# Start addresses of weight and moving tiles in a two-layer fp32 decoder kernel: distance 0 for products of 512 columns, 64 for products of 256

## The chip, the core and the metric

The kernel runs on one core of one Trainium2 chip. The metric is the device time of one execution in microseconds (us); lower is better. Of the kernel before, three runs are known: 1990.70, 1990.41 and 1990.72 us, median 1990.7.

## The reference

Two layers over 512 tokens of width 1024, all in float32. Each layer is a half-step gated feed-forward network (FFN), a mixer, a second FFN and a gated per-layer input. The mixer of layer 0 is a convolution module, that of layer 1 a sparse attention. Cut to what matters here:

```python
for i in range(2):
    x = x + 0.5 * swiglu(rms_norm(x, ffn1_norm[i]), ffn1_w_gate[i], ffn1_w_up[i], ffn1_w_down[i])
    h = rms_norm(x, mix_norm[i])
    x = x + (conformer_conv(h, ...) if i == 0 else nsa_mixer(h, ...))
    x = x + 0.5 * swiglu(rms_norm(x, ffn2_norm[i]), ffn2_w_gate[i], ffn2_w_up[i], ffn2_w_down[i])
    gate = sigmoid(rms_norm(x, ple_norm[i]) @ ple_w_gate[i])
    x = x + gate * (p[i] @ ple_w_in[i])
return rms_norm(x, final_norm)

def swiglu(x, wg, wu, wd):                 # x 512x1024, wg and wu 1024x2816, wd 2816x1024
    return (silu(x @ wg) * (x @ wu)) @ wd
```

## The kernel before

Everything is kept transposed: a tile has 128 features in its partitions and the 512 tokens along a row. A float32 value is split into a high part, rounded to the type that TensorE multiplies in one pass (fp32r), and a low part, the rest. A product of float32 matrices is then three matmuls, issued by `mm3` (lines 361 to 365): weights high with moving high (L363), weights high with moving low (L364), weights low with moving high (L365). Each matmul is a weight load of 128x128 (PEld in the profile) and the pass of the moving operand over it (PE). The load for the next matmul runs during the pass of this one.

There are two widths of moving operand.

- **Products of 512 columns**: one matrix block against all tokens. The down projections of the FFNs (moving tiles `hid`), the first two gate and up blocks of each FFN, the convolution module's projections (moving tiles `s`, and `tw` for the second one), the per-layer input (`px`, `zp`), the attention's projections (`s`, and `e` for part of its output), and the attention's own scores (`kt` against weights `q`) and weighted sums (`t` and `ect` against weights `v` and `vc`).
- **Products of 256 columns**: the other gate and up blocks. `pairs` (its copies and additions are L509 and L510; `ffn` calls it) works on two blocks of 128 output features at once with a seven-product scheme, in which a product takes sums of blocks and half of the tokens. Per pair of blocks the names `s`, `c`, `e`, `d` stand for the four kinds of weights: the block itself, its two sums, and the sum `s1hl`, which is kept in a tile of its own. The moving operands are halves of `s` or `px` tiles (columns 0 to 255, or 256 to 511). In the final stage (`final`) the last three blocks of the last gate also go by halves of 256 columns.

An FFN runs in three parts of 8, 8 and 6 blocks (`PARTS`). Each part is gate and up, then the down projection of these blocks into the accumulated result. So on TensorE a stretch of 256-column products is followed by one of 512-column products, three times per FFN; the first part of an FFN begins with four plain 512-column blocks.

Weights come from memory by DMA into `raw` tiles of 128x1024, are split by ScalarE (`wh`, L299) and VectorE (`wl`, L301), and stay in a ring of five pairs of tiles (`HLB`). A tile holds eight 128-column blocks; a matmul reads one block, 512 bytes of each partition.

**Where the tiles lie.** A pool's tiles lie one after another in each partition, in the order in which their tags are first used, and every start is a multiple of 32 bytes. For this text the *distance* of a matmul is the start of its weights minus the start of its moving operand, modulo 256 bytes. (The words of the change count it the other way, moving minus weights: their 192 is 64 here.) As blocks are 512 bytes apart and halves 1024, all products of a kind of tile have one distance. In the kernel before three paddings are set by hand (`PAD_SLOTS`, `PAD_PHASE`, `PADS`), and the starts modulo 256 are: `wh`, `wl` 192; `s`, `px` 0; `hid` 192; `s1hl` 64; `tw` 224; `zp` 96; `t` 0 against `v` 224. That gives these distances:

| products | columns | matmuls | distance before | distance after |
|---|---|---|---|---|
| `s`, `px` with `wh`, `wl` | 256 | 5,904 | 192 | 64 (144 of the final stage: 0) |
| `px` with `s1hl` | 256 | 960 | 64 | 64 |
| `hid` with `wh`, `wl` | 512 | 2,112 | 0 | 0 |
| `s`, `px` with `wh`, `wl` | 512 | 1,656 | 192 | 0 |
| `tw` with `wh`, `wl` | 512 | 192 | 224 | 0 |
| `zp` with `wh`, `wl` | 512 | 96 | 96 | 0 |
| `e` with `wh`, `wl` | 512 | 96 | eight values, 0 to 224 | 0 |
| `t` with `v`; `ect` with `vc` | 512 | 160; 32 | 224; 0 | 0; 0 |
| `kt` with `q` | 512 | 64 | 160 or 32 | 0 |

The engines take their instructions in the order of the program, as the scheduler has laid it down; each waits for its operands by semaphores.

Of the kernel before, what the change touches and what calls it, by code (L numbers as in the profile page):

```python
# [21 lines left out]
TAPS = 31  # L22
X_W1, WARM = 4, 18
OUTS = 2
PAD_SLOTS, PAD_PHASE = 16, 48
PADS = {"s1hl": 16, "G": 48, "hid": 48}
CONV_FIN = 0
PE_LATE = (3, 4, 5)
FIN_PRI = 100
# [16 lines left out]
EB = 9  # L46
# [151 lines left out]
class Kern:  # L198
    def __init__(self, ctx, tc, aps):
        self.ctx, self.tc, self.nc = ctx, tc, tc.nc  # L200
        self.a = aps
        pool = lambda name, **kw: ctx.enter_context(tc.tile_pool(name=name, **kw))
        self.cpool = pool("consts", bufs=1)
        self.wpool = pool("weights", bufs=1)
        pool("gap0", bufs=1).tile([128, PAD_SLOTS], F32, name="gap0")
        self.spool = pool("slots", bufs=1)
        self.tiny = pool("tiny", bufs=2)
        pool("gap1", bufs=1).tile([128, PAD_PHASE], F32, name="gap1")
        self.ppool = pool("ps", bufs=1, space=PSUM)
# [13 lines left out]
    def tmp(self, dt=F32):  # L223
        return self.ptile("t", self.tb, dt=dt)

    def ptile(self, tag, n, w=512, dt=F32):
        if tag in PADS and tag not in self.padded:
            self.padded.add(tag)
            self.phase.tile([128, PADS[tag]], F32, name=f"gap{tag}{self.uid}", tag=f"gap{tag}", bufs=1)
        self.uid += 1  # L230
        return self.phase.tile([128, w], dt, name=f"{tag}{self.uid}", tag=tag, bufs=n)

# [34 lines left out]
        name, i = UNITS[j][0][0][:2]  # L267
        return (name[:4], i) == self.now

    def halves(self):  # L270
        h = self.wpool.tile([128, HU], F32R, name=f"wh{self.uid}", tag="wh", bufs=self.HLB)
        l = self.wpool.tile([128, HU], F32R, name=f"wl{self.uid}", tag="wl", bufs=self.HLB)
        self.uid += 1
        return h, l

    def _split(self, what, j):
        nc = self.nc
        w = sum(x[2] for x in UNITS[j])
        if what == "r":
            t = self.wpool.tile([128, HU], F32, name=f"wr{j}", tag="wh", bufs=self.HLB)  # L280
            nc.sync.dma_start(t[:, :w], self.a["w"][j, :, :w])
            self.hl[j] = (t, t)
            return
        if what in "cd":
            self.combine(what, j)
            return
        pair = KINDS[j] == "a"
        t = self.raw[j]
        if KINDS[j] == "s":
            del self.raw[j]  # L290
        h, l = self.halves()
        name = UNITS[j][0][0][0]
        nsa, calm = name.startswith("nsa"), name.startswith(CALM)
        eng = nc.gpsimd if calm or nsa and j % 4 in L_POOL else nc.vector
        for c in self.pieces(j, w):
            if nsa and j % 4 in H_POOL:
                nc.gpsimd.tensor_copy(h[:, c], t[:, c])
            else:
                nc.scalar.activation(h[:, c], t[:, c], AF.Copy)  # L299
            with self.behind() if pair else nullcontext():  # L300
                eng.tensor_tensor(l[:, c], t[:, c], h[:, c].bitcast(F32), op=OP.subtract)  # L301
        self.hl[("s", j) if pair else j] = (h, l)
        if pair:
            with self.behind():
                self.first_sums(j)
# [5 lines left out]
    def combine(self, what, j):  # L311


        nc = self.nc
        t, u = self.raw[j], self.raw[j + 1]
        lo, hi = slice(0, HU // 2), slice(HU // 2, HU)
        q = self.sums[j]
        if what == "c":
            nc.vector.tensor_tensor(q[:, lo], u[:, lo], t[:, lo], op=OP.subtract)
            nc.vector.tensor_tensor(u[:, lo], t[:, hi], q[:, lo], op=OP.subtract)  # L320
        src = q if what == "c" else u
        h, l = self.halves()
# [396 lines left out]
    def glu(self, c, pa, pg, ta=None):  # L719

        nc = self.nc
        if ta is None:
            ta = self.scaled(pa)
        with self.tc.high_priority(FIN_PRI):
            nc.vector.tensor_tensor(pg, pg, self.R, op=OP.mult)
            nc.scalar.activation(pg, pg, AF.Sigmoid, bias=self.col("conv_b_pw1", KD + c))
            if CONV_ON[c] == "pe":
                u = self.ptile("uu", 2, PH * (SP + LAGS - 1)).rearrange("p (q s) -> p q s", q=PH)
                nc.gpsimd.memset(u[:, :, :LAGS - 1], 0.0)
                nc.vector.scalar_tensor_tensor(ta, ta, self.col("conv_b_pw1", c), pg, op0=OP.add, op1=OP.mult)  # L730
                nc.sync.dma_start(self.ud[c * 128:c * 128 + 128, :], ta)
                nc.sync.dma_start(u[:, :, LAGS - 1:], self.byphase(self.ud, c))
            else:
                u = self.ptile("u", 3, S + TAPS - 1)
# [103 lines left out]
    def conv(self, nxt):  # L838

        nc = self.nc  # L840
        X, U, Y = self.X, {}, []
        self.dwc = self.phase.tile([128, KD, TAPS], F32, name="dwc")
# [159 lines left out]
    def put_k(self, g):  # L1002
        nc, t, KT = self.nc, self.kt, self.KTs[g % 2]
        for br, sl, ot in ((0, slice(0, 64), slice(64, 128)), (1, slice(64, 128), slice(0, 64))):
            nc.scalar.activation(KT[sl, 0, br, 32:], t[sl], AF.Copy)
            nc.vector.tensor_tensor(KT[sl, 1, br, 32:], t[sl], KT[sl, 0, br, 32:].bitcast(F32), op=OP.subtract)
            nc.sync.dma_start(KT[ot, :, br, 32:].bitcast(F32), KT[sl, :, br, 32:].bitcast(F32))

    def kc_into(self, g):
        nc, KT = self.nc, self.KTs[g % 2]  # L1010
# [3 lines left out]
    def proj_q(self, g, pr):  # L1014
# [6 lines left out]
        Q = self.phase.tile([128, 2, 512], F32R, name=f"q{g}{pr}", tag="q", bufs=4)  # L1021
# [60 lines left out]
    def cmp_in(self, j, first):  # L1082
# [14 lines left out]
            next(fin)  # L1097
        for gp, p in wait:
            for s in range(2):
                t = self.ptile("e", EB, 516)  # L1100
# [54 lines left out]
    def scores(self, job):  # L1155
# [15 lines left out]

        for a in range(HPG):
            Q = self.Q[g, a // 2][:, a % 2, qt * 128:qt * 128 + 128]
            src, e = {}, self.slot() if a == HPG - 1 else self.ptile("e", EB, 516)
            if len(brs) == 2:
                p = self.bank()
                for i in range(2):
# [106 lines left out]
    def osplit(self, g):  # L1284
        nc = self.nc
        for pr in range(2):
            t = self.OT[g][pr]
            h, l = (self.slot(F32R) if g < 2 else self.ptile("e", EB, 516, F32R)[:, :512] for _ in range(2))
            nc.scalar.activation(h, t, AF.Copy)
            nc.vector.tensor_tensor(l, t, h.bitcast(F32), op=OP.subtract)  # L1290
            self.OS[g * 2 + pr] = (h, l)
# [23 lines left out]
    def nsa(self, nxt):  # L1315
        nc = self.nc
        self.TT, self.Q, self.J, self.OT, self.OS = {}, {}, {}, {}, {}
        self.pend = []
        P = self.phase
# [3 lines left out]
        self.pos = P.tile([128, 2, 16], F32, name="pos")  # L1323
        nc.gpsimd.dma_start(self.pos, self.a["pos"])
        self.rowmask = P.tile([128, 1], F32, name="rowmask")
        nc.gpsimd.dma_start(self.rowmask, self.a["rowmask"])
        self.gates = P.tile([128, 4, 48], F32, name="gates")
        self.gates0 = P.tile([128, 16], F32, name="gates0")
        self.kc = P.tile([128, G, 32], F32, name="kc")
        self.ec = P.tile([128, 4, HPG, 32], F32, name="ec")  # L1330
        nc.gpsimd.memset(self.ec, 0.0)
        self.vc = P.tile([128, G, 128], F32R, name="vc")
        self.KTs = [P.tile([128, 2, 2, 544], F32R, name=f"kt{i}") for i in range(2)]
        self.Vs = [P.tile([128, 8, 128], F32R, name=f"v{i}") for i in range(2)]
        self.ects = [P.tile([128, 2, 512], F32R, name=f"ect{i}") for i in range(2)]
        for t in self.KTs:
            nc.gpsimd.memset(t[:, :, 0, :32].bitcast(F32), 0.0)
        for t in self.ects:
# [201 lines left out]
```

## Time and profile before

| | |
|---|---|
| device time, three runs | 1990.70, 1990.41, 1990.72 us |
| the profiled execution: device time | 1990.31 us |
| the profiled execution: first to last instruction (span) | 1988.2 us |
| mean granted TensorE clock | 0.997 |
| PE, PEld busy | 1961.4 us (99%), 1760.0 us (89%) |
| DVE, ACT, POOL busy | 1544.6 us (78%), 1099.8 us (55%), 331.0 us (17%) |

The profile calls TensorE's matmuls PE and its weight loads PEld; DVE is VectorE, ACT ScalarE, POOL GpSimd, SP the engine that issues most DMAs. Matmuls are pipelined: a row gives each one a length of 0.28 us (256 columns) or 0.39 us (512 columns), and the next one starts long before this one's end. What a matmul costs on TensorE is therefore not its length but the time from its start to the start of the next. This text calls that the *pitch* and takes it from rows of the timeline: the first and last start of a gapless run, over the number of steps between them. In the views by windows, "x152" behind the busy time counts the matmuls that overlap the window.

### The profile page before, as it was taken

Reading aid. Unit: us, or ns where it says so; the run is one execution under the profiler, and the core shown is the slowest. Engines: PE = TensorE matmul, PEld = TensorE weight load, DVE = VectorE, ACT = ScalarE, POOL = GpSimd, SP = SyncE. Lnnn points to the kernel's source line nnn. Section 1 sums busy time; section 2 is a strip of 40 time slices with the busy share of each in tenths; the row PEclk is TensorE's granted clock in tenths of the full one; section 3 lists DMA queues with packets and bytes.
Section 4 is the critical chain, followed back from the end, with each engine's and each line's share of the span. In section 5 each row is a group of like instructions: output and inputs, shape, how many; then the busy total and the mean of one; then the engine's idle time right before and its main releaser. Section 6 shows DMA issues by size and latency. Waiting matters only on the chain.

```text
span 1988.2 us, 32709 instructions
## 1 busy us (share of the span) xinstructions
PE 1961.4 (99%) x12534; PEld 1760.0 (89%) x12534; DVE 1544.6 (78%) x2703; ACT 1099.8 (55%) x1972; POOL 331.0 (17%) x365
## 2 busy tenths in 40 slices
PE   8999999999999999999999999999999999999998
PEld 7989898888789898988999989888888789998987
DVE  8869777795688796877978868636889797786875
ACT  7636446663565363545644626337888665363543
POOL 0000000352300000022000000557666200000022
PEclk9999999999999999999999999999999999999999
DMA  4332322566425243343232323463332023232241
GB/s 172 107 106 97 128 86 96 192 206 202 138 99 172 88 151 128 99 138 117 85 126 87 129 84 100 156 196 106 89 96 101 23 94 129 96 117 96 96 149 53
DMA packets 79483, 235.16 MB, mean 118 GB/s; under 512 B 8848, under 2 KB 16160, under 8 KB 79328
## 3 DMA queue, kind: packets, MB, share of 16 engines
q1 hardware_dynamic: 78368, 230.69, 35.4%
q8 instruction: 98, 1.61, 0.3%
q0 software_dynamic: 816, 2.33, 0.3%
q14 instruction: 57, 0.47, 0.1%
q10 hardware_dynamic: 144, 0.07, 0.0%
HBM read 214.66 MB, written 16.29 MB: 116 GB/s over the span
## 4 chain that ended last, share of the span: by engine, by line
PE 90%; DVE 6%; ACT 1%; issue 1%; DMA 1%; SPq 0%; POOL 0%; DVEq 0%; ACTq 0%; POOLq 0%
PE b L363 27%; PE b L364 27%; PE b L365 27%; PE b L828 2%; PE b L1187 1%; PE b L1251 1%; DMA raw<-in_w 1%; PE b L1270 1%; PE b L1271 1%; PE b L1126 1%; DVE s L422 1%; DVE t L489 1%; DVE wl L301 1%; DVE px L498 0%; DVE acc L439 0%
## 5 line engine op out<-in xcount | busy, mean ns | idle before, releaser
L363 PE MATMUL b<-s,wh 128*128 128x256 f32 (+1 forms) x1408 | 443.8, 316 | 2.2 <-ACT wh L299 1.4
L364 PE MATMUL b<-s,wh 128*128 128x256 f32 (+1 forms) x1408 | 440.9, 314 | 1.4 <-DVE s L422 1.2
L365 PE MATMUL b<-s,wl 128*128 128x256 f32 (+1 forms) x1408 | 440.2, 314 | 0.1
L299 ACT ACTIVATE wh<-raw 128x1024 fp32r<-128x1024 f32 (+1 forms) x251 | 263.7, 1053 | 241.8 <-PE b L364 158.4
L364 PE MATMUL b<-px,wh 128*128 128x256 f32 (+1 forms) x1112 | 319.8, 288 | 1.7 <-DVE px L498 1.7
L363 PE MATMUL b<-px,wh 128*128 128x256 f32 (+1 forms) x1112 | 319.4, 288 | 0.7 <-ACT G L510 0.7
L365 PE MATMUL b<-px,wl 128*128 128x256 f32 (+1 forms) x1112 | 319.6, 288 | 0.0
L301 DVE TENSOR_TENSOR wl<-raw,wh 128x1024 fp32r<-128x1024 f32 (+1 forms) x205 | 251.6, 1229 | 65.2 <-ACT wh L299 64.8
L363 PEld LDWEIGHTS b<-s,wh 128*128 128x128 f32 x1408 | 264.5, 188 | 21.2 <-ACT wh L299 2.2
L364 PEld LDWEIGHTS b<-s,wh 128*128 128x128 f32 x1408 | 264.3, 188 | 20.4 <-DVE s L422 2.3
L365 PEld LDWEIGHTS b<-s,wl 128*128 128x128 f32 x1408 | 263.4, 188 | 18.6 <-DVE wl L301 0.5
L364 PE MATMUL b<-hid,wh 128*128 128x512 f32 x704 | 273.1, 389 | 0.0
L365 PE MATMUL b<-hid,wl 128*128 128x512 f32 x704 | 272.7, 389 | 0.0
L363 PE MATMUL b<-hid,wh 128*128 128x512 f32 x704 | 269.1, 389 | 0.0
L301 POOL TENSOR_TENSOR wl<-raw,wh 128x1024 fp32r<-128x1024 f32 (+1 forms) x53 | 128.5, 2429 | 695.2 <-ACT wh L299 695.1
L510 ACT ACTIVATE G<-b 128x256 f32<-128x256 f32 x400 | 144.5, 376 | 132.4 <-PE b L365 109.8
L364 PEld LDWEIGHTS b<-px,wh 128*128 128x128 f32 x1112 | 208.7, 188 | 7.1 <-DVE px L498 2.3
L363 PEld LDWEIGHTS b<-px,wh 128*128 128x128 f32 x1112 | 208.4, 188 | 6.1 <-ACT G L510 1.3
L365 PEld LDWEIGHTS b<-px,wl 128*128 128x128 f32 x1112 | 208.8, 188 | 4.0
L364 PEld LDWEIGHTS b<-hid,wh 128*128 128x128 f32 x704 | 132.1, 188 | 27.0
L365 PEld LDWEIGHTS b<-hid,wl 128*128 128x128 f32 x704 | 132.0, 188 | 27.1
L363 PEld LDWEIGHTS b<-hid,wh 128*128 128x128 f32 x704 | 132.1, 188 | 26.9
(246 smaller groups left out, 3621.0 us busy)
## 6 DMA issues: line engine op xcount, KB each, us to landing
raw<-in_w SPq DMA_DIRECT2D x255, 512.0 KB, 3.3
rawx<-in_w SPq DMA_DIRECT2D x80, 512.0 KB, 3.3
tw<-in_tw SPq DMA_DIRECT2D x20, 576.0 KB, 6.6
skew<-table SPq DMA_DIRECT2D x16, 320.0 KB, 5.8
z<-t SPq DMA_DIRECT2D x16, 256.0 KB, 2.4
hid<-z SPq DMA_DIRECT2D x16, 256.0 KB, 3.9
tt<-skew SPq DMA_DIRECT2D x16, 256.0 KB, 2.9
wr<-in_w SPq DMA_DIRECT2D x8, 512.0 KB, 4.0
```

Source lines behind the costliest of these rows:

```text
L299: nc.scalar.activation(h[:, c], t[:, c], AF.Copy)
L301: eng.tensor_tensor(l[:, c], t[:, c], h[:, c].bitcast(F32), op=OP.subtract)
L363: mm(out, sh, mh, start=start, stop=False, **how)
L364: mm(out, sh, ml, start=False, stop=False, **how)
L365: self.lastmm = mm(out, sl, mh, start=False, stop=stop, **how).ins
L422: b = nc.vector.scalar_tensor_tensor(view(l), x, g, view(h.bitcast(F32)), op0=OP.mult, op1=OP.subtract)
L489: sub = lambda o, x, y: nc.vector.tensor_tensor(o, x, y, op=OP.subtract)
L510: copy = lambda o, x: nc.scalar.activation(o, x, AF.Copy)
L828: nc.tensor.matmul(p[:, q * SP:q * SP + SP], T[q][:, d * 128:d * 128 + 128], u[:, q, o:o + SP], start=d == 0, stop=d == LAGS - 1)
L1126: nc.tensor.matmul(P[mh][:, :124], w, B[kk // 4][:, kk % 4, :], start=kk == 0, stop=kk == 15)
L1187: nc.tensor.matmul(p[:, :32 - lo + nk], Q, KT[:, i, "sw".index(b), lo:32 + nk], start=i == 0, stop=i == 1)
L1251: nc.tensor.transpose(p[:, a * 128:a * 128 + 128], J[a, b][:, kt * 128:kt * 128 + 128], self.ident)
```

## The change

It sets where tiles lie. No instruction is added, removed or moved: on each of the five engines the program holds the same instructions in the same order, with other addresses.

- The pool `tiny` is taken before the weights, with one padding of 128 bytes, so that `raw`, `wh`, `wl`, `wr` and `s` tiles start at 128 modulo 256.
- `halves` makes each weight tile 64 columns wider. Weights for 256-column pairs use it from column 16 on (`TURN`), so they start at 192; all others from column 0, so they start at 128.
- `ptile` and the new `own` count the bytes that the phase's pool has given out (`self.top`) and put a padding ahead of a tag's first tile, so that it starts at the value in `AT` or in the call of `own`: `px`, `hid`, `tw`, `e`, `kt` at 128, `s1hl` at 192, `tt`, `q`, `vc`, `v`, `ect` at 0. The tiles of other tags follow on.
- Rows whose length was no multiple of 256 bytes become 576 columns (`UW`): `u`, `uu`, `e`, `kt`. What is read and written in them stays the same.

```diff
-PAD_SLOTS, PAD_PHASE = 16, 48
-PADS = {"s1hl": 16, "G": 48, "hid": 48}
+PAD, TURN = 32, 16
+AT = {"s1hl": 192, "px": 128, "hid": 128, "tw": 128, "e": 128, "tt": 0, "q": 0}
+UW = 576
...
         self.cpool = pool("consts", bufs=1)
+        self.tiny = pool("tiny", bufs=2)
+        pool("gap0", bufs=1).tile([128, PAD], F32, name="gap0")
         self.wpool = pool("weights", bufs=1)
-        pool("gap0", bufs=1).tile([128, PAD_SLOTS], F32, name="gap0")
         self.spool = pool("slots", bufs=1)
-        self.tiny = pool("tiny", bufs=2)
-        pool("gap1", bufs=1).tile([128, PAD_PHASE], F32, name="gap1")
...
+    def place(self, tag, size, at=None):
+        pad = 0 if at is None else (at - self.top) % 256
+        if pad:
+            self.uid += 1
+            self.phase.tile([128, pad // 4], F32, name=f"gap{tag}{self.uid}", tag=f"gap{tag}", bufs=1)
+        self.top += pad + -(-size // 32) * 32
...
     def ptile(self, tag, n, w=512, dt=F32):
-        if tag in PADS and tag not in self.padded:
-            self.padded.add(tag)
-            self.phase.tile([128, PADS[tag]], F32, name=f"gap{tag}{self.uid}", tag=f"gap{tag}", bufs=1)
+        if tag not in self.tags:
+            self.tags.add(tag)
+            self.place(tag, n * (-(-w * 4 // 32) * 32), AT.get(tag))
...
-    def halves(self):
-        h = self.wpool.tile([128, HU], F32R, name=f"wh{self.uid}", tag="wh", bufs=self.HLB)
-        l = self.wpool.tile([128, HU], F32R, name=f"wl{self.uid}", tag="wl", bufs=self.HLB)
+    def halves(self, half=False):
+        o = TURN if half else 0
+        h = self.wpool.tile([128, HU + 64], F32R, name=f"wh{self.uid}", tag="wh", bufs=self.HLB)[:, o:o + HU]
+        l = self.wpool.tile([128, HU + 64], F32R, name=f"wl{self.uid}", tag="wl", bufs=self.HLB)[:, o:o + HU]
...
-        h, l = self.halves()
+        h, l = self.halves(pair)
...
-        h, l = self.halves()
+        h, l = self.halves(True)
...
-            nc.scalar.activation(KT[sl, 0, br, 32:], t[sl], AF.Copy)
+            nc.scalar.activation(KT[sl, 0, br, 32:544], t[sl], AF.Copy)
...
-        self.vc = P.tile([128, G, 128], F32R, name="vc")
-        self.KTs = [P.tile([128, 2, 2, 544], F32R, name=f"kt{i}") for i in range(2)]
-        self.Vs = [P.tile([128, 8, 128], F32R, name=f"v{i}") for i in range(2)]
-        self.ects = [P.tile([128, 2, 512], F32R, name=f"ect{i}") for i in range(2)]
+        self.vc = self.own("vc", [128, G, 128], F32R, at=0)
+        self.KTs = [self.own(f"kt{i}", [128, 2, 2, UW], F32R, at=128) for i in range(2)]
+        self.Vs = [self.own(f"v{i}", [128, 8, 128], F32R, at=0) for i in range(2)]
+        self.ects = [self.own(f"ect{i}", [128, 2, 512], F32R, at=0) for i in range(2)]
...
         def phase():
-            self.padded = set()
+            self.tags, self.top = set(), 128
```

More of the change, by code (lines that the diff above doesn't have):

```diff
@@ L224, in tmp, with own @@
         return self.ptile("t", self.tb, dt=dt)
+    def place(self, tag, size, at=None):
[4 more added lines that the diff above has]
+        self.top += pad + -(-size // 32) * 32
+    def own(self, name, shape, dt=F32, at=None):
+        size = 4
+        for n in shape[1:]:
+            size *= n
+        self.place(name, size, at)
+        return self.phase.tile(shape, dt, name=name)
     def ptile(self, tag, n, w=512, dt=F32):
-        if tag in PADS and tag not in self.padded:
-            self.padded.add(tag)
-            self.phase.tile([128, PADS[tag]], F32, name=f"gap{tag}{self.uid}", tag=f"gap{tag}", bufs=1)
+        if tag not in self.tags:
+            self.tags.add(tag)
+            self.place(tag, n * (-(-w * 4 // 32) * 32), AT.get(tag))
         self.uid += 1
@@ L279, in _split @@
         if what == "r":
-            t = self.wpool.tile([128, HU], F32, name=f"wr{j}", tag="wh", bufs=self.HLB)
+            t = self.wpool.tile([128, HU + 64], F32, name=f"wr{j}", tag="wh", bufs=self.HLB)[:, :HU]
             nc.sync.dma_start(t[:, :w], self.a["w"][j, :, :w])
@@ L727, in glu @@
             if CONV_ON[c] == "pe":
-                u = self.ptile("uu", 2, PH * (SP + LAGS - 1)).rearrange("p (q s) -> p q s", q=PH)
+                u = self.ptile("uu", 2, UW)[:, :PH * (SP + LAGS - 1)].rearrange("p (q s) -> p q s", q=PH)
                 nc.gpsimd.memset(u[:, :, :LAGS - 1], 0.0)
@@ L733, in glu @@
             else:
-                u = self.ptile("u", 3, S + TAPS - 1)
+                u = self.ptile("u", 3, UW)[:, :S + TAPS - 1]
                 nc.gpsimd.memset(u[:, :TAPS - 1], 0.0)
@@ L841, in conv @@
         X, U, Y = self.X, {}, []
-        self.dwc = self.phase.tile([128, KD, TAPS], F32, name="dwc")
+        self.dwc = self.own("dwc", [128, KD, TAPS])
         nc.gpsimd.dma_start(self.dwc, self.a["dwc"])
@@ L1004, in put_k @@
         for br, sl, ot in ((0, slice(0, 64), slice(64, 128)), (1, slice(64, 128), slice(0, 64))):
-            nc.scalar.activation(KT[sl, 0, br, 32:], t[sl], AF.Copy)
-            nc.vector.tensor_tensor(KT[sl, 1, br, 32:], t[sl], KT[sl, 0, br, 32:].bitcast(F32), op=OP.subtract)
-            nc.sync.dma_start(KT[ot, :, br, 32:].bitcast(F32), KT[sl, :, br, 32:].bitcast(F32))
+            nc.scalar.activation(KT[sl, 0, br, 32:544], t[sl], AF.Copy)
+            nc.vector.tensor_tensor(KT[sl, 1, br, 32:544], t[sl], KT[sl, 0, br, 32:544].bitcast(F32), op=OP.subtract)
+            nc.sync.dma_start(KT[ot, :, br, 32:544].bitcast(F32), KT[sl, :, br, 32:544].bitcast(F32))
     def kc_into(self, g):
@@ L1020, in proj_q @@
         nc.vector.tensor_tensor(l, t, h.bitcast(F32), op=OP.subtract)
-        Q = self.phase.tile([128, 2, 512], F32R, name=f"q{g}{pr}", tag="q", bufs=4)
+        Q = self.ptile("q", 4, 1024, F32R).rearrange("p (a n) -> p a n", a=2)
         lo, hi = slice(0, 64), slice(64, 128)
@@ L1099, in cmp_in @@
             for s in range(2):
-                t = self.ptile("e", EB, 516)
+                t = self.ptile("e", EB, UW)
                 o = 1 - s
@@ L1173, in scores @@
             Q = self.Q[g, a // 2][:, a % 2, qt * 128:qt * 128 + 128]
-            src, e = {}, self.slot() if a == HPG - 1 else self.ptile("e", EB, 516)
+            src, e = {}, self.slot() if a == HPG - 1 else self.ptile("e", EB, UW)
             if len(brs) == 2:
@@ L1287, in osplit @@
             t = self.OT[g][pr]
-            h, l = (self.slot(F32R) if g < 2 else self.ptile("e", EB, 516, F32R)[:, :512] for _ in range(2))
+            h, l = (self.slot(F32R) if g < 2 else self.ptile("e", EB, UW, F32R)[:, :512] for _ in range(2))
             nc.scalar.activation(h, t, AF.Copy)
@@ L1318, in nsa @@
         self.pend = []
-        P = self.phase
         self.xd = self.dpool.tile([D, S], F32, name="xd")
@@ L1322, in nsa @@
             nc.gpsimd.dma_start(self.xd[m * 128:m * 128 + 128, :], self.xs[m])
-        self.pos = P.tile([128, 2, 16], F32, name="pos")
+        self.pos = self.own("pos", [128, 2, 16])
         nc.gpsimd.dma_start(self.pos, self.a["pos"])
-        self.rowmask = P.tile([128, 1], F32, name="rowmask")
+        self.rowmask = self.own("rowmask", [128, 1])
         nc.gpsimd.dma_start(self.rowmask, self.a["rowmask"])
[L1327 to L1330, printed above, removed]
+        self.gates = self.own("gates", [128, 4, 48])
+        self.gates0 = self.own("gates0", [128, 16])
+        self.kc = self.own("kc", [128, G, 32])
+        self.ec = self.own("ec", [128, 4, HPG, 32])
         nc.gpsimd.memset(self.ec, 0.0)
-        self.vc = P.tile([128, G, 128], F32R, name="vc")
-        self.KTs = [P.tile([128, 2, 2, 544], F32R, name=f"kt{i}") for i in range(2)]
-        self.Vs = [P.tile([128, 8, 128], F32R, name=f"v{i}") for i in range(2)]
-        self.ects = [P.tile([128, 2, 512], F32R, name=f"ect{i}") for i in range(2)]
+        self.vc = self.own("vc", [128, G, 128], F32R, at=0)
+        self.KTs = [self.own(f"kt{i}", [128, 2, 2, UW], F32R, at=128) for i in range(2)]
+        self.Vs = [self.own(f"v{i}", [128, 8, 128], F32R, at=0) for i in range(2)]
+        self.ects = [self.own(f"ect{i}", [128, 2, 512], F32R, at=0) for i in range(2)]
         for t in self.KTs:
```

## The prediction

> **What bounds the kernel now.** I read the page first: its span, the busy shares and the chain that ended last.
>
> ```profile
> span 1988.2 us, 32709 instructions
> PE 1961.4 (99%) x12534; PEld 1760.0 (89%) x12534; DVE 1544.6 (78%) x2703; ACT 1099.8 (55%) x1972; POOL 331.0 (17%) x365
> PE 90%; DVE 6%; ACT 1%; issue 1%; DMA 1%; SPq 0%; POOL 0%; DVEq 0%; ACTq 0%; POOLq 0%
> ```
>
> TensorE works almost without a gap, and 90% of the chain is its own. No instruction moves, so the time can change only through the pitch of the matmuls. The groups by shape give the counts. The three lines L363 to L365 have equal counts, so each row stands for three times as many.
>
> ```profile
> L364 PE MATMUL b<-px,wh 128*128 128x256 f32 x1008 | 278.9, 277 | 1.7 <-DVE px L498 1.7
> L364 PE MATMUL b<-s,wh 128*128 128x256 f32 x960 | 265.1, 277 | 0.0
> L364 PE MATMUL b<-px,s1hl 128*128 128x256 f32 x320 | 88.1, 277 | 0.2 <-DVE px L498 0.2
> L364 PE MATMUL b<-s,wh 128*128 128x512 f32 x448 | 175.9, 393 | 1.4 <-DVE s L422 1.2 <-DVE s L1290 0.2
> L364 PE MATMUL b<-px,wh 128*128 128x512 f32 x104 | 40.9, 393 | 0.0
> L364 PE MATMUL b<-tw,wh 128*128 128x512 f32 x64 | 25.1, 395 | 0.0
> L364 PE MATMUL b<-zp,wh 128*128 128x512 f32 x32 | 12.7, 396 | 0.0
> L1270 PE MATMUL b<-t,v 128*128 128x512 f32 x80 | 34.4, 430 | 0.8 <-ACT t L1253 0.7
> ```
>
> That makes 3 x (1008 + 960 + 320) = 6,864 products of 256 columns, and 3 x (448 + 104) = 1,656 of 512 columns with `s` or `px` that stand at distance 192. The mean lengths hide pipelining, so the pitches come from the timeline, as first and last start of gapless runs. First, 512 columns at distance 0 (`hid`, 159 steps); then the same width at distance 192 (`px`, then `s`, 154 steps).
>
> ```profile
> 1797.83 0.39 PE L363 MATMUL b<-hid,wh 128*128 128x512 f32 x1
> ...
> 1833.87 0.39 PE L363 MATMUL b<-hid,wh 128*128 128x512 f32 x1
> ```
>
> ```profile
> 909.61 0.39 PE L365 MATMUL b<-px,wl 128*128 128x512 f32 x1
> ...
> 944.86 0.39 PE L363 MATMUL b<-s,wh 128*128 128x512 f32 x1
> ```
>
> 36.04 us / 159 = 226.7 ns, against 35.25 / 154 = 228.9 ns. Operation, shape and clock are the same, and each run is gapless: 2.2 ns go with the addresses. Products with `tw`, at distance 224, take longer still (8 steps):
>
> ```profile
> 534.63 0.39 PE L363 MATMUL b<-tw,wh 128*128 128x512 f32 x1
> ...
> 536.50 0.39 PE L365 MATMUL b<-tw,wl 128*128 128x512 f32 x1
> ```
>
> 1.87 / 8 = 233.8 ns, 7.1 above `hid`. The 256-column products are different: they go at one of two pitches. Two runs of the same mix of tiles, each with both distances in it, first 146 steps and then 151:
>
> ```profile
> 1628.20 0.28 PE L365 MATMUL b<-px,wl 128*128 128x256 f32 x1
> ...
> 1645.39 0.28 PE L365 MATMUL b<-px,s1hl 128*128 128x256 f32 x1
> ```
>
> ```profile
> 1728.79 0.28 PE L363 MATMUL b<-px,s1hl 128*128 128x256 f32 x1
> ...
> 1745.90 0.28 PE L363 MATMUL b<-px,wh 128*128 128x256 f32 x1
> ```
>
> 17.19 / 146 = 117.7 ns, and 17.11 / 151 = 113.3 ns, which is half of 226.7. I call them the long and the short pitch; the long one costs 4.4 ns a product. Once at the short pitch, a run keeps it across changes of distance; the long one holds too. The long pitch comes with the entry: after a stretch of 512-column products, the second and third part of every FFN (eight parts) begin with it and keep it for some 8.4 us, about 72 products, until the first `s1hl` product, the first at distance 64. The first and the last of these eight stretches, and the sum over all long-pitch stretches of the execution, by windows:
>
> ```profile
> 141.26:149.70 8.44, 8.44 (x73) 1.00 0.37 124
> ...
> 1838.60:1847.05 8.45, 8.45 (x73) 1.00 0.37 125
> ...
> sum 197.05, PE 195.36; mean PE 8.49
> ```
>
> So 195.4 us of TensorE's time pass at the long pitch, 195.4 / 0.1177 = 1,660 products, and 195.4 x (117.7 - 113.3) / 117.7 = 7.3 us is all that the short one could still bring.
>
> **Part by part. 512 columns to distance 0.** `hid` shows that a run at distance 0 holds 226.7. The 1,656 `s` and `px` products gain 2.2 ns: 3.6 us. The 3 x 64 with `tw` gain 7.1: 1.4. The 3 x 32 with `zp` stand at distance 96, which is in neither run; between 2.2 and 7.1 ns they give 0.2 to 0.7; I take 0.6, near `tw`, since the mean lengths are alike (396 and 395 ns, against 393 for `s`). In the attention stand 352 more (`t`, `ect`, `e` and `kt` in the table of distances), of which a run of `t` with `v` shows a pitch:
>
> ```profile
> 1397.74 0.39 PE L1271 MATMUL b<-t,v 128*128 128x512 f32 x1
> 1397.97 0.39 PE L1270 MATMUL b<-t,v 128*128 128x512 f32 x1
> ```
>
> 230 ns at distance 224. These stand singly between other kinds, and a change of kind costs time of its own, so I take 0 to 7.1 ns, 0 to 2.5 us, and 1.5 as the value. Together 7.1 us, if TensorE alone sets the pace. In the attention it doesn't quite:
>
> ```profile
> 1240.00:1360.00 120.00, 118.92 (x618) 100.16 (x617) 62.19 (x108) 49.32 (x85) 65.92 (x80) 1.00 0.52 162
> 1360.00:1480.00 120.00, 119.08 (x646) 99.92 (x645) 102.02 (x430) 101.89 (x319) 86.12 (x115) 1.00 0.34 97
> 1480.00:1600.00 120.00, 114.64 (x577) 93.25 (x577) 100.85 (x368) 91.35 (x271) 52.30 (x86) 0.99 0.23 78
> ```
>
> The columns are PE, PEld, DVE, ACT and POOL; from 1360 us on DVE and ACT are busy 76 to 85% and TensorE pauses for 6.3 us. The groups of these 360 us show how many of the `s` products lie there:
>
> ```profile
> L363 PE MATMUL b<-s,wh 128*128 128x512 f32 x208 | 83.2, 403 | 0.1
> ```
>
> 3 x 208 = 620 products, 1.4 us of the gain, and with the 1.5 above 2.9. I give back half of that, since the value that DVE or ACT makes next then comes late instead. **512 columns: 7.1 - 1.4 = 5.7 us faster.** Ends: 3.9 (nothing in the attention and 0.2 for `zp`: 2.3 + 1.4 + 0.2) and 8.2 (3.6 + 1.4 + 0.7 + 2.5).
>
> **256 columns to distance 64.** What a long run at 64 does is not in the trace; only runs of 24 `s1hl` products at most are. Two rows bear on it, one for each side. For: in the eight parts above the step to 64 ended the long pitch within two products, while none of the eight runs at 192 left it by itself in 72 products. The end of one such stretch, where the pitch falls from 118 to 113 ns:
>
> ```profile
> 688.59 0.28 PE L363 MATMUL b<-px,wh 128*128 128x256 f32 x1
> 688.71 0.28 PE L364 MATMUL b<-px,wh 128*128 128x256 f32 x1
> 688.83 0.28 PE L365 MATMUL b<-px,wl 128*128 128x256 f32 x1
> 688.94 0.28 PE L363 MATMUL b<-px,s1hl 128*128 128x256 f32 x1
> 689.06 0.28 PE L364 MATMUL b<-px,s1hl 128*128 128x256 f32 x1
> 689.17 0.28 PE L365 MATMUL b<-px,s1hl 128*128 128x256 f32 x1
> ```
>
> Against: in the first part of the last FFN 24 `s1hl` products at 64 kept the long pitch from end to end (2.70 us over 23 steps):
>
> ```profile
> 1642.69 0.28 PE L363 MATMUL b<-px,s1hl 128*128 128x256 f32 x1
> ...
> 1645.39 0.28 PE L365 MATMUL b<-px,s1hl 128*128 128x256 f32 x1
> ```
>
> So the long pitch is possible at 64; the question is how a run enters. The likelier reading is that at 64 a disturbed start settles at the short one, since the step from 192 to 64 is such a disturbance and mostly did. Then all 7.3 us are there to gain, except where something else is the bound. That is the first part of the last FFN:
>
> ```profile
> 1613.00:1662.00 49.00, 47.55 (x395) 46.67 (x394) 48.83 (x73) 32.98 (x53) 0.00 (x0) 1.00 0.34 110
> ```
>
> DVE, the third busy column, is busy 48.8 of 49.0 us, so the 47.6 x 4.4 / 117.7 = 1.8 us that TensorE would save there turn into waiting for DVE. I take off 0.2 more for entries. **256 columns: 7.3 - 1.8 - 0.2 = 5.3 us faster.** Ends: 7.3 faster; the other end is the second rival.
>
> **All else.** Paddings and longer rows move no byte more by DMA or engine, and no instruction or wait. The 144 products of the final stage that come to distance 0 with 256 columns have no row; at 4.4 ns each way they are 0.6 us at most, and I take 0.
>
> **Sum.** 5.7 + 5.3 = 11.0 us. The profiled execution took 1990.31 us, 2.1 more than its span, and lies 0.4 below the median of 1990.7. 1990.3 - 11.0 = 1979.3; against the median 1979.7. The forecast is 1979.7 us.
>
> **Rivals.** *Only 512 columns gain (0.12).* The 256-column products keep their share at the long pitch: 1990.7 - 5.7 = 1985.0. For it: a pitch holds once entered, whatever the distance; against: the eight ends at `s1hl`.
>
> *Locked at the long pitch: the rival on the other side (0.17).* If the entry from 512 columns gives the long pitch at 64 as it does at 192, nothing ends it: the end came with a step from 192 to 64, and after the change there is no such step. It then lasts to each part's end. The 6,864 - 1,660 = 5,200 products that now have the short pitch pay 4.4 ns, 22.9 us; less 5.7 that is 17.2 us slower: 1990.7 + 17.2 = 2007.9. It decides from 11.0 / 0.0044 = 2,500 long-pitch products on, a third of all: fewer, and the change still gains. For it speaks the run of 24; against it, the ends.
>
> *Some parts lock (0.12).* A third to half of the products at the long pitch: 1987 to 1994, middle 1990.
>
> *Addresses don't matter (0.04).* The long pitch and the 2.2 ns would then come from the neighbours of a stage, not from the distance, and the time stays 1990.7. Against it: `hid` holds 226.7 wherever it stands, `px` and `s` 228.9. The Trainium skill, "TensorE: Matmul & The Clock Gate", section "Step-by-step: what each phase is for", says this outright: TensorE has two independent read ports, and "Loading the next tile's weights doesn't steal SBUF read bandwidth from the running matmul". By that rule the sum would be 0; the trace, with 226.7 against 228.9 ns at one shape, disagrees.
>
> **How the numbers follow.** The forecast has 0.55. A measurement of this kernel can tell about 0.2%, 4 us, from no change. Faster than 1986.7: the forecast and the first rival, 0.67. Within 0.2%: some parts locked and addresses without effect, 0.16. Slower: locked, 0.17. The range leaves out the locked case alone, 0.17: from 1976 (8.2 us on 512 columns and 6.4 on 256, with half of the 1.8 behind DVE gained after all: 1990.7 - 14.6) to 1994, the upper end of some parts locked.
>
> **What would show it.** In the profile after, right steps would be: `s` and `px` runs of 512 columns and `tw` runs at 226.7 ns; the first 72 products of each later FFN part at 113.3; the first part of the last FFN hardly shorter, with more waiting for DVE. Wrong: 256-column runs at 117.7 that last to the end of a part (locked), or runs of 512 columns at distance 0 that still take 229 or more.

## The result and the profile after

The changed kernel takes 2010.49 us (median of five runs, 2008.1 to 2012.63) against 1990.7 us for the kernel before on the same chip (five runs, 1990.41 to 1991.97). The ratio is 1.0098, with a 95% interval of 1.0083 to 1.0113: it is slower by 1%, where 1979.7 us was forecast. The profiled execution took 2012.63 us. Its page, with the rows that answer to those of before:

```profile
span 2010.5 us, 32709 instructions
PE 1980.5 (99%) x12534; PEld 1783.0 (89%) x12534; DVE 1546.1 (77%) x2703; ACT 1101.0 (55%) x1972; POOL 337.8 (17%) x365
PE 90%; DVE 6%; ACT 2%; issue 1%; POOL 1%; DMA 0%; SPq 0%; DVEq 0%; POOLq 0%; ACTq 0%
```

TensorE is as full as before and works 19 us longer with the same matmuls. So the pitches tell the story, as the prediction said. The same runs of 512 columns as there, now at distance 0: `px`, then `s` (154 steps), and `tw` (8 steps), first and last start:

```profile
919.08 0.39 PE L380 MATMUL b<-px,wl 128*128 128x512 f32 x1
...
953.98 0.39 PE L378 MATMUL b<-s,wh 128*128 128x512 f32 x1
```

```profile
539.13 0.39 PE L378 MATMUL b<-tw,wh 128*128 128x512 f32 x1
...
540.95 0.39 PE L380 MATMUL b<-tw,wl 128*128 128x512 f32 x1
```

34.90 us / 154 = 226.6 ns and 1.82 / 8 = 227.5 ns, the 226.7 of `hid` within what two digits show. The 512-column half of the change does what it says. The 256-column half does the reverse. These are the first and the last product of the second part of the first FFN, 671 steps apart:

```profile
143.12 0.28 PE L378 MATMUL b<-s,wh 128*128 128x256 f32 x1
...
222.15 0.28 PE L380 MATMUL b<-px,wl 128*128 128x256 f32 x1
```

79.03 / 671 = 117.8 ns: the long pitch from the entry to the end. The eight later parts by windows (span of the window, then PE) are all alike, and none has a gap:

```profile
143.12:222.15 79.03, 79.03 (x673) 79.03 (x671) 66.45 (x95) 46.42 (x78) 0.00 (x0) 1.00 0.34 113
265.81:325.05 59.24, 59.24 (x504) 59.24 (x503) 47.76 (x68) 34.16 (x57) 0.00 (x0) 1.00 0.29 98
...
1858.47:1917.71 59.24, 59.24 (x504) 59.24 (x503) 47.77 (x68) 34.01 (x57) 0.00 (x0) 1.00 0.29 98
sum 553.07, PE 553.07 PEld 553.06 DVE 457.21 ACT 322.88 POOL 0.00; mean PE 69.13 PEld 69.13 DVE 57.15 ACT 40.36 POOL 0.00
```

Before, only the first 72 or so products of each of these parts had the long pitch.

There is a third difference, which nothing in the prediction speaks of. Near 957 us, in the first FFN of the second layer, GpSimd's power (`r<-v,power`, the inverse root of the norm) took far longer, and TensorE waited for it. First before, then after; the last number in brackets is the wait and what ended it:

```profile
948.15 1.39 POOL L445 TENSOR_TENSOR r<-v,power 128x4 f32<-128x4 f32 x1 [35.53 <-DVE v L474]
```

```profile
957.38 8.81 POOL L460 TENSOR_TENSOR r<-v,power 128x4 f32<-128x4 f32 x1 [35.28 <-DVE v L489]
...
966.24 0.47 PE L473 MATMUL b<-ident,r 128*128 128x128 f32 x1 [3.66 <-POOL r L460]
```

In windows with the same work, before and then after (span, PE, PEld, DVE, ACT, POOL, clock, DMA share, GB/s):

```profile
940.40:959.30 18.90, 18.90 (x91) 15.65 (x90) 17.68 (x31) 13.36 (x21) 1.39 (x1) 1.00 0.00 0
```

```profile
950.00:975.00 25.00, 21.34 (x89) 17.34 (x88) 20.08 (x34) 13.23 (x21) 8.81 (x1) 0.86 0.09 29
```

TensorE pauses for 3.7 us, and the granted clock, 1.00 before, falls to 0.86 over the window (half clock for 6.8 us). From the same product to the same product it is 25.2 us after against 18.8 before, 6.5 us.

As the order of the instructions is the same, every product can be set against itself: the sum over products of pitch after minus pitch before. By kind that gives, for differences under 16 ns, +19.7 us for the products of 256 columns and -4.8 us for those of 512; the larger differences at the power's stall add 6.5 us. That is 21.4 of the 22.3 us between the two profiled executions; the medians lie 19.8 apart.

### The profile page after: what moved, and what is told of

Same layout as the page of the kernel before. It is cut to its first block, busy times and chain, and to the rows that moved or that the text cites. A ratio compares the mean times of both kernels' runs of the same rounds, so it can differ in the third digit from the quotient of the medians.

```text
span 2010.5 us, 32709 instructions
## 1 busy us (share of the span) xinstructions
PE 1980.5 (99%) x12534; PEld 1783.0 (89%) x12534; DVE 1546.1 (77%) x2703; ACT 1101.0 (55%) x1972; POOL 337.8 (17%) x365
## 4 chain that ended last, share of the span: by engine, by line
PE 90%; DVE 6%; ACT 2%; issue 1%; POOL 1%; DMA 0%; SPq 0%; DVEq 0%; POOLq 0%; ACTq 0%
PE b L378 27%; PE b L379 27%; PE b L380 27%; PE b L843 2%; PE b L1202 1%; PE b L1266 1%; PE b L1285 1%; PE b L1286 1%; PE b L1141 1%; DVE t L504 1%; DVE s L437 1%; DVE wl L316 1%; DVE px L513 1%; DVE acc L454 0%; DMA raw<-in_w 0%
## 5 line engine op out<-in xcount | busy, mean ns | idle before, releaser
L379 PE MATMUL b<-px,wh 128*128 128x256 f32 (+1 forms) x1112 | 323.3, 291 | 1.6 <-DVE px L513 1.6
L378 PE MATMUL b<-px,wh 128*128 128x256 f32 (+1 forms) x1112 | 322.8, 291 | 0.7 <-ACT G L525 0.7
```

Of the source, the lines that this page charges most:

```text
L378: mm(out, sh, mh, start=start, stop=False, **how)
L379: mm(out, sh, ml, start=False, stop=False, **how)
```

## The experiments

Two questions stood open: what ends the long pitch, and, once it was ended, why the time didn't fall below that of before. All kernels at a glance. "Long" is how many products of each later part ran at the pitch of the entry before 113.3 ns came; "power" is the duration of the power near 945 to 964 us; the ratio is to the kernel before on the same chip, with its 95% interval, where the kernel was timed more than once.

| kernel | distance of pairs / `s1hl` | long | power, us | time, us | ratio |
|---|---|---|---|---|---|
| before | 192 / 64 | about 72 | 1.39 | 1990.7 | |
| the change | 64 / 64 | all | 8.81 | 2010.5 | 1.0098 (1.0083 to 1.0113) |
| w192_s64 | 192 / 64 | 71 to 75 | 8.81 | 1992.8 | 1.0011 (1.0002 to 1.0021) |
| all192 | 192 / 192 | all | 8.81 | 2011.9 | 1.0108 (1.0093 to 1.0124) |
| w64_s192 | 64 / 192 | 95 or 96 | 8.82 | 1990.8 | 1.0005 (0.9996 to 1.0014) |
| before_pairs64 | 64 / 64 | all | 1.39 | 2010.0 | 1.0096 (1.0081 to 1.0112) |
| all_at_128 | 128 / 128 | all, at 120.0 | 8.81 | 2025.5 | one run |
| gate_at_192 | 192, then 64 / 64 | 24 to 27 | 8.81 | 1987.3 | 0.9987 (0.9978 to 0.9996) |
| tiny_back | 64 / 192 | 95 or 96 | 8.81 | 1989.9 | 0.9999 (0.9991 to 1.0008) |
| before_tiny_first | 192 / 64 | about 72 | 1.39 | 1989.4 | 1.0000 (0.9991 to 1.0009) |
| dve_tiles_old | 192, then 64 / 64 | 24 to 27 | 8.81 | 1989.8 | 1.0001 (0.9992 to 1.0010) |
| raw_old | 192, then 64 / 64 | 24 to 27 | 8.81 | 1988.6 | one run |
| t_old | 192, then 64 / 64 | 24 to 27 | 8.81 | 1988.0 | one run |
| sums_plus_1 | 192, then 64 / 64 | 24 to 27 | 1.39 | 1982.4 | 0.9963 (0.9949 to 0.9976) |
| sums_plus_4 | 192, then 64 / 64 | 24 to 27 | 9.41 | 1989.6 | one run |

### What ends the long pitch

**w192_s64**: the changed kernel with the pairs' distances of before.

```diff
-PAD, TURN = 32, 16
+PAD, TURN = 32, 48
```

> The changed kernel with the pairs' weights from column 48 on: wh and wl at distance 192 again, s1hl at 64, 512 columns at 0. Entry theory (a run of 256 columns that follows a settled run of 512 at distance 0 begins at the long pitch of 117.7 ns, and only a step of distance from 192 to 64 ends it): 72 long products at the start of each later FFN part, then 113.3 ns; all but the 5.7 us on 512 columns as before the change: 1985.0 us. Distance theory (the long pitch belongs to 64, the short one to 192): nearly no long pitch, about 1980. Address theory (the new base of 128 and the wider tiles hold the long pitch, not the missing step): still some 2008.

The long pitch was back to 71 to 75 products per later part, as expected, and 18 us went. The time is 1992.8 and not 1985. Some 2.5 us of that are longer 256-column products, in first parts of the FFNs that stayed long and in the final stage; the rest, some 5 us, is the 512-column gain, which isn't seen in the time. That is the second question.

**all192**: one distance again, but 192.

```diff
-PAD, TURN = 32, 16
-AT = {"s1hl": 192, ...
+PAD, TURN = 32, 48
+AT = {"s1hl": 64, ...
```

> The changed kernel with every 256-column product of the pairs at distance 192, s1hl too: one constant distance, as in the change, but another. Entry theory: no step, so the long pitch lasts to the end of each later FFN part, 672 and 504 products: 2008. Distance theory: short pitch throughout, 1980.

```profile
142.78 0.28 PE L378 MATMUL b<-s,wh 128*128 128x256 f32 x1
...
221.81 0.28 PE L380 MATMUL b<-px,wl 128*128 128x256 f32 x1
```

79.03 us over 671 steps, to the hundredth the same as with 64 in the change. So 64 isn't a bad distance and 192 a good one; with one distance throughout, the later parts, which have no gap, stay long at either.

**w64_s192**: the pairs stay at 64, `s1hl` goes to 192, so that the steps come the other way round.

```diff
-AT = {"s1hl": 192, ...
+AT = {"s1hl": 64, ...
```

> The changed kernel with s1hl alone moved, to distance 192; all other 256-column products stay at 64. The first block of a part meets a step from 64 to 192 at product 73 and one back to 64 at about 97. Entry theory: long pitch up to the step back, 96 products instead of 72, then short: 1985.0 + 8 x 24 x 4.4 ns = 1986. Distance theory: only the 960 products with s1hl change, by 4.4 ns: 2008 - 4 = 2004.

The rows at the beginning and the end of the first `s1hl` block of a part, and the part's last product:

```profile
149.59 0.28 PE L380 MATMUL b<-px,wl 128*128 128x256 f32 x1
149.71 0.28 PE L378 MATMUL b<-px,s1hl 128*128 128x256 f32 x1
...
152.42 0.28 PE L380 MATMUL b<-px,s1hl 128*128 128x256 f32 x1
152.54 0.28 PE L378 MATMUL b<-px,wh 128*128 128x256 f32 x1
152.65 0.28 PE L379 MATMUL b<-px,wh 128*128 128x256 f32 x1
152.76 0.28 PE L380 MATMUL b<-px,wl 128*128 128x256 f32 x1
...
217.70 0.28 PE L380 MATMUL b<-px,wl 128*128 128x256 f32 x1
```

The step from 64 to 192 at 149.71 changes nothing: (152.42 - 149.71) / 23 = 117.8 ns. The step from 192 to 64 at 152.54 ends it: (217.70 - 152.54) / 575 = 113.3 ns. The direction counts, and the end of the long pitch follows the step, after 96 products here as after 72 before.

**before_pairs64**: the kernel before, where only the pairs' weight tiles go 32 columns on, from 192 to 64. All products of 512 columns keep their old distances.

```diff
-    def halves(self):
+    def halves(self, half=False):
+        o = 32 if half else 0
...
+        h = self.wpool.tile([128, HU + 64], F32R, name=f"wh{self.uid}", tag="wh", bufs=self.HLB)[:, o:o + HU]
```

> The kernel before the change with one edit: the pairs' weights lie 128 bytes further on, so that all 256-column products stand at distance 64; 512 columns as they were. Entry theory: no step any more, long pitch to the end of each part, 5,200 products more at 4.4 ns: 1990.7 + 22.9 = 2013.6. Address theory: as before the change, about 1990.7, since bases and other tiles stay. If the loss came from the 512-column part of the change instead: 1990.7 or less.

2010.0 us: this one edit costs 19 us by itself, and all eight later parts stay long. It kept the power at 1.39 us, which was the first hint that the stall belongs to something else. Three of the four first parts, which come here from 512-column products at distance 192, went at 113.3 ns from their second product on (two of them until a wait): the step from 192 to 64 can lie at the entry itself. The fourth (585.18 us) was long to its end.

**all_at_128**: one distance that no other kernel has.

```diff
-PAD, TURN = 32, 16
-AT = {"s1hl": 192, ...
+PAD, TURN = 32, 32
+AT = {"s1hl": 0, ...
```

> The changed kernel with all 256-column products of pairs at one distance, 128, which no run has had. Entry theory: no step, so the long pitch from the first to the last product of each part as with 64 and with 192, near 2010. Rival, a good distance: at half of 256 the products settle short by themselves, 113.3 ns from the first on and near 1985 to 1990.

```profile
142.93 0.29 PE L378 MATMUL b<-s,wh 128*128 128x256 f32 x1
...
223.45 0.29 PE L380 MATMUL b<-px,wl 128*128 128x256 f32 x1
```

80.52 / 671 = 120.0 ns, longer than the long pitch, and from end to end. The expectation of "near 2010" was too low by 15 us; no good distance was found either.

**gate_at_192**: if a step from 192 to 64 is what ends it, it can come at once. The first weights of every gate stand at 192, everything else at 64.

```diff
-        o = TURN if half else 0
+        o = half or 0
...
-        h, l = self.halves(pair)
+        h, l = self.halves(pair and (48 if UNITS[j][0][0][0].endswith("gate") else TURN))
...
-        h, l = self.halves(True)
+        h, l = self.halves(TURN)
```

> The changed kernel with one edit: the pair tiles of the gate's first weights stand at column 48 (distance 192), all other pair tiles and s1hl stay at 64. So every group of products starts with 24 products at 192 and steps to 64 after them. Entry theory (a part enters at the long pitch and a step from 192 to 64 ends it, no step the other way does): 24 to 30 long products per part where w64_s192 had 95, then 113.3 ns; with (95-24) x 8 x 4.4 ns = 2.5 us less than w64_s192: 1988.3, the stall of the power on GpSimd still in it. Rival: the step only counts between tiles of the weights and s1hl (another tile, another writer), and not within the weights: long all through as in the change, 2010.

```profile
142.07 0.28 PE L378 MATMUL b<-s,wh 128*128 128x256 f32 x1
...
144.89 0.28 PE L378 MATMUL b<-s,wh 128*128 128x256 f32 x1
145.01 0.28 PE L379 MATMUL b<-s,wh 128*128 128x256 f32 x1
145.13 0.28 PE L380 MATMUL b<-s,wl 128*128 128x256 f32 x1
145.25 0.28 PE L378 MATMUL b<-s,wh 128*128 128x256 f32 x1
...
218.23 0.28 PE L380 MATMUL b<-px,wl 128*128 128x256 f32 x1
```

(144.89 - 142.07) / 24 = 117.5 ns up to the step, then (218.23 - 145.25) / 644 = 113.3. Step and short pitch lie within the same tag of tiles, so `s1hl` plays no part of its own. What the 256-column products take above 113.3 ns fell from 7.5 us in the kernel before to 3.6.

A step isn't the only thing that can change the pitch: a wait of TensorE can do it at one distance. In the changed kernel, the first part of the second layer's first FFN, all at 64:

```profile
974.92 0.28 PE L378 MATMUL b<-s,wh 128*128 128x256 f32 x1
...
986.58 0.28 PE L380 MATMUL b<-px,wl 128*128 128x256 f32 x1
987.10 0.38 PE L378 MATMUL b<-px,wh 128*128 128x256 f32 x1 [0.24 <-ACT G L525]
...
987.44 0.28 PE L380 MATMUL b<-px,wl 128*128 128x256 f32 x1
...
1024.73 0.28 PE L380 MATMUL b<-px,wl 128*128 128x256 f32 x1
```

(986.58 - 974.92) / 99 = 117.8 ns up to the wait, (1024.73 - 987.44) / 329 = 113.3 from there to the end of the part. It isn't sure to happen: in all192 the same products kept 117.8 ns across the same wait, and in before_pairs64 the waits near 1639 us turned a part from 113.3 to 117.8. The eight later parts have no such wait, so there the steps alone decide.

### Where the 512-column gain went

In every kernel with the new placement the products of 512 columns took 3.6 to 4.1 us above 226.7 ns where before had 8.6, and yet those in which the long pitch ended early were not 5 us faster than before. Product by product against before, gate_at_192 gains 2.9 us between 350 and 600 us (the convolution), and gives 5.0 back between 950 and 1000, at the power.

**tiny_back** and **before_tiny_first**: the place of the small tiles `v` and `r`. The first is w64_s192 with them behind the slots, the second the kernel before with them ahead of the weights; paddings keep all other starts modulo 256.

```diff
-        self.tiny = pool("tiny", bufs=2)
         pool("gap0", bufs=1).tile([128, PAD], F32, name="gap0")
         self.wpool = pool("weights", bufs=1)
         self.spool = pool("slots", bufs=1)
+        self.tiny = pool("tiny", bufs=2)
+        pool("gap1", bufs=1).tile([128, GAP], F32, name="gap1")
```

> The 512-column products kept their gain at distance 0 in every kernel with the new placement, and yet none of them is faster than before; in all four of them the fifth power on GpSimd (r<-v,power, near 945 to 957 us) took 8.81 us where the two kernels with the old placement show 1.39. This is w64_s192 (median 1990.8) with the small tiles v and r behind the slots again, as before; every other tile keeps its address modulo 256, so all distances of matrix products stay. If the place of these tiles makes the stall: the power takes 1.4 us, no half clock near 955 us, and about 5.5 us go: 1985.3. If the stall belongs to something else in the new placement (the gaps, the weights' rows, the order of the engines' work): 8.8 us again and 1990.8.

> The kernel before with the small tiles ahead of the weights, as the change has them, and all else at its old address modulo 256. If the place of the small tiles alone makes the stall of the power: 8.8 us in place of 1.39, and 1990.7 + 5.5 = 1996.2. If it takes the rest of the new placement too, or comes from something else: 1.4 us and 1990.7.

8.81 us in the first, 1.39 in the second: the place of these tiles is not the cause.

**dve_tiles_old**, **raw_old**, **t_old**: gate_at_192 with the addresses of VectorE's own tiles as before, all and by halves.

```diff
-AT = {..., "tt": 0, "q": 0}
+AT = {..., "tt": 0, "q": 0, "t": 0, "rawx": 0, "sq": 0, "G": 0}
...
-            t = self.wpool.tile([128, HU], F32, name=f"raw{j}", tag="raw", bufs=2)
+            t = self.wpool.tile([128, HU + 64], F32, name=f"raw{j}", tag="raw", bufs=2)[:, 16:16 + HU]
```

> gate_at_192 (median 1987.3) with VectorE's own tiles back at their old addresses modulo 256: raw at 192, rawx, sq, t and G at 0; the distances of all pair products and of nearly all products of 512 columns stay (98 of those that read t go to 128). In all seven kernels with the new placement the power on GpSimd took 8.81 us and ended 0.87 us after VectorE's unbroken run of instructions ended; in the three with the old placement it took 1.39 us within an equally unbroken run. Port theory: VectorE keeps GpSimd out of the memory while it reads two operands at some relative addresses; with the old ones back the power takes 1.4 us and the stall's 5 us go: 1982.3. Rival: the moment at which the power is issued decides (the changed pace of TensorE), not VectorE's addresses: 8.8 us and 1987.3.

> The half of dve_tiles_old with raw at 192 and rawx and sq at 0, t and G as in the change. By the port theory 1.4 us if the difference of two weight tiles (sq<-rawx,raw is what VectorE runs as the power starts) is what keeps GpSimd out, 8.8 us if it is t<-G,t, which comes next. By the rival of the moment 8.8 us.

> The other half of dve_tiles_old: t and G at 0, raw, rawx and sq as in the change. By the port theory 1.4 us if t<-G,t is what keeps GpSimd out, 8.8 us if it is the difference of two weight tiles. By the rival of the moment 8.8 us.

8.81 us in all three, and 1989.8 us in place of 1982.3: the theory of VectorE's addresses, the one called the port theory there, has fallen too. What was left shows in VectorE's rows: the instruction ahead of `v`, and `v`, in the timeline of the kernel before and then of gate_at_192.

```profile
947.24 0.69 DVE L498 TENSOR_TENSOR px<-t,px 128x512 fp32r<-128x512 f32 x1
947.91 0.16 DVE L474 TENSOR_SCALAR v<-b 128x4 f32<-128x4 f32 x1
```

```profile
943.78 0.68 DVE L513 TENSOR_TENSOR px<-t,px 128x512 fp32r<-128x512 f32 x1
944.38 0.15 DVE L489 TENSOR_SCALAR v<-b 128x4 f32<-128x4 f32 x1
```

VectorE's instructions normally overlap: the next starts some 0.08 us before the end of the last. Before, `v` starts 0.67 us after `px`, in gate_at_192 0.60: so before, `v` came 0.07 us late, since it waited for TensorE's column sums. My reading was that TensorE, with 226.7 ns in place of 228.9, is now ahead and the wait gone; the next two kernels test it.

**sums_plus_1** and **sums_plus_4** bring the wait back with all addresses as in gate_at_192: in this one FFN one of the four column sums, or all four, are made twice (and, by the same edit, those of the norm behind it, near 1275 us). The diff is that of sums_plus_1.

```diff
-        for q in range(p.shape[1]):
+        for q in (*range(p.shape[1]), *((3,) if self.now == ("ffn1", 1) else ())):
```

> gate_at_192 (median 1987.3) with one of the four column sums ahead of v made twice in ffn1 of the second layer (two more rows on TensorE, some 0.22 us), so that v comes later against VectorE. In the three kernels without the stall VectorE waited for the sums before v (v starts 12 to 17 ns before the instruction ahead of it ends), in the ten with it it did not (76 to 84 ns before that end: the usual overlap). Theory of the moment: with the wait back the power gets in at once, 1.4 us, no half clock near 955 us, and the time falls by the stall's 5.0 us less 0.2: 1982.5. Rival (anything fixed in the new placement): 8.8 us or more (the order puts two more instructions into VectorE's run, 1.1 us), 1987.5 to 1988.5.

> The same with all four sums made twice (0.9 us later). Theory of the moment: VectorE waits longer still, the power takes 1.4 us, near 1983. Rival: 8.8 us, 1988.

The timeline of sums_plus_1, first VectorE and then GpSimd, and the window of the same work as above (span, PE, PEld, DVE, ACT, POOL, clock):

```profile
942.65 0.68 DVE L513 TENSOR_TENSOR px<-t,px 128x512 fp32r<-128x512 f32 x1
943.34 0.16 DVE L489 TENSOR_SCALAR v<-b 128x4 f32<-128x4 f32 x1
```

```profile
943.58 1.39 POOL L460 TENSOR_TENSOR r<-v,power 128x4 f32<-128x4 f32 x1 [35.36 <-DVE v L489]
```

```profile
935.80:954.70 18.90, 18.90 (x92) 15.84 (x91) 17.68 (x31) 13.36 (x21) 1.39 (x1) 1.00 0.00 0
```

`v` starts 0.69 us after `px`, the power takes 1.39 us, TensorE has no pause and the full clock, and the median is 1982.43 us (1980.82 to 1984.69; the kernel before beside it 1990.65), where 1982.5 was expected. In the two profiled executions, 5.3 us of the gain over gate_at_192 lie between the start of the second part of the first FFN and the first pair product behind the power, which is where the stall was. sums_plus_4 missed its expectation and still speaks for the same theory: the scheduler set `v` two instructions later in VectorE's order, behind the sums, so there was no wait (0.08 us of overlap), and with four extra sums in it the power took 9.41 us:

```profile
944.30 9.41 POOL L460 TENSOR_TENSOR r<-v,power 128x4 f32<-128x4 f32 x1 [36.19 <-DVE v L489]
```

So the extra rows on TensorE don't cure the stall; in these kernels it goes with the wait at `v`. In sums_plus_4 the instruction behind `v` is another one too. sums_plus_1 beats both kernels, by 0.37% over before (0.24 to 0.51).

## Why the prediction was wrong, point by point

- **What bounds the kernel.** Right: TensorE, by its pitches. It missed that a product is set off by chains through other engines, one of which stands on the edge.
- **512 columns, the pitch.** Right: `s`, `px` and `tw` at 226.7 ns. The rule of the Trainium skill weighed there ("TensorE: Matmul & The Clock Gate", section "Step-by-step: what each phase is for"), that a weight load takes no read bandwidth from the running matmul, would have them where they were, if it is read as the prediction read it (it speaks of read bandwidth, and the prediction's "outright" for addresses goes further than that); the same products at the same clock got shorter by their addresses alone, so the trace disagrees with that reading for these operands.
- **512 columns, the sum.** 7.1 us ahead of the give-back was too much; product by product it is 4.8: `s` and `px` 2.4 (3.6 was put down), `tw` 1.25 (1.4), `zp` 0.5 (0.6), the attention's own products 0.6 (1.5). The 2.2 ns of one run were taken for all 1,656, but the 633 `s` products of the attention gained only 0.85 ns each. (3 x 208 there is 624 and not 620, which changes no figure.)
- **The give-back of 1.4 us in the attention** did not come: between 1240 and 1600 us the products are 0.9 us shorter in all. Instead 5 us or more were given back where none were looked for, at the power.
- **256 columns: the step that failed.** "The likelier reading is that at 64 a disturbed start settles at the short one, since the step from 192 to 64 is such a disturbance and mostly did." The evidence for the short pitch at 64 was always evidence for a *step* to 64. A distance of 64 alone did not bring it: the change takes away the steps and with them the only thing that had ended the long pitch in the eight later parts (the change, all192, before_pairs64: all long; w192_s64, w64_s192, gate_at_192: long up to the step).
- **The rival that came true** is "locked at the long pitch": "nothing ends it", with 2007.9 us. Its mechanism was right. Its 22.9 us are 19.7 in the trace: the eight parts have 672 or 504 products each, 4,704, of which 8 x 72 were long already; 4,128 x 4.4 = 18.2 us, the final stage adds 0.8, and in the first parts of the FFNs losses and gains nearly cancel. The stall costs 6.5 us in the profiled execution and 5.0 in gate_at_192, where the half clock behind it was shorter (3.4 us against 6.8): 1990.7 + 19.7 - 4.8 + 5.0 to 6.5 is 2010.6 to 2012.1, against 2010.5.
- **The first part of the last FFN.** The 1.8 us taken off for VectorE were not lost: between 1600 and 1700 us the 256-column products became 1.4 us shorter. The part entered long, as before, and went short behind waits of TensorE some 100 products in, at one distance, which the prediction did not foresee.
- **The 144 products of the final stage** were put at 0 with 0.6 as the end. They cost 0.83 us: at distance 0 they have 120 ns, as the pairs had at 128, a pitch of which no row of before told.
- **Addresses don't matter**: fallen, as foreseen.

The long pitch alone sets the sign. With the step put back, gate_at_192 has 1987.3 us; without the stall as well, sums_plus_1 comes within 3 us of the forecast.

## What to carry to other kernels

A pitch that a trace shows ended by an event is evidence for the event, not for what holds afterwards: before the event is taken away, ask what else would end it. When matmuls get faster, list the chains through other engines that end just in time, since 0.07 us of lead was enough here to turn a gain of 5 us into nothing. Comparing two executions instruction by instruction, where the order is the same, finds such a place at once, while the shares of busy time don't show it.

## What the runs showed of the hardware that was not expected

- Two pitches at one distance. A stretch of fp32r matmuls of 256 columns that comes without a gap after 512-column ones at distance 0, as in the eight later parts, runs at 117.8 ns with distance 64 or 192, and at 120.0 with 128, for as long as 671 steps. A step from 192 to 64 brings 113.3, which then holds through steps both ways; the step from 64 to 192 did not bring it. Nor is the step needed: a wait of 0.24 us brought 113.3 at distance 64. A step is not enough everywhere: in the first part of the last FFN of the kernel before, and in three first parts of w192_s64 after waits had made them long again, such products stayed long across one or two of the steps, until the one at product 396. What in TensorE keeps the two apart isn't shown by any run.
- A tiny instruction on GpSimd can be kept waiting until VectorE runs out of work. In all eleven kernels with the stall the power ended 0.87 us after the end of VectorE's unbroken run of instructions (7.94 us after the power's start, 8.54 in sums_plus_4), most of which read two tiles. That run ended because its next instruction, `b<-b,R`, itself needs what the power makes (`R` is spread from `r`; in the change it starts at 968.02 us after 2.71 us of waiting for `R`), so its place in VectorE's order bounds the stall. What an earlier place would bring was not tried. The Trainium skill, "GPSIMD Engine Reference", section "8. Key points", says that GpSimd shares its memory interfaces with VectorE and contends with instructions of two inputs there. That agrees with the end of the stall, but that section doesn't say when it happens: in the four kernels without it the power took 1.39 us within a run just as unbroken, which went on for 12 us more.
- The wait at `v` isn't the whole condition either. In gate_at_192 the power at 565.82 us found VectorE in an unbroken run, with no wait at `v`, and took 1.41 us; other instructions followed `v` there (`px<-t,px` and not the difference of two weight tiles or a `wl`). Whether the instruction behind `v` decides was not tried. So at this place the wait is shown to decide, in kernels with the same addresses (one sum more on TensorE and, behind the power, two of VectorE's instructions in another order are the other differences of sums_plus_1 there; a second sum near 1275 us and another order of some instructions from the second layer's mixer on come later), and the rule behind it stays open.
